# Output-weight sums in a hybrid attention layer: from accumulating DMAs to VectorE additions spread over three stages

## The chip, the cores and the metric

The kernel runs on one core of a Trainium2 chip. The metric is the device time of one execution in microseconds. The kernel before was timed in three runs; its time is their median. One further execution was profiled, and every row below is from that one.

## The reference

The reference is one layer of a streaming encoder: 16 learned meta tokens are put ahead of 512 positions of width 2048, and then

```python
u = rms_norm(h, pre_w)
proj = u @ w_in          # q, latent kv, gate, indexer for A; q, k, v, gate for B; two merge gates
# A: indexer scores, top-k keys per query, attention in the compressed space, 8 heads
# B: softmax(q1 k1 + bias) - lam * softmax(q2 k2 + bias) over a chunk mask, 8 heads, norm per head
y_a = (o_a * silu(z_a)) @ w_o_a
y_b = (o_b * silu(z_b)) @ w_o_b
mix = sigmoid(g_a) * y_a + sigmoid(g_b) * y_b
out = mix @ w_out
return h + rms_norm(out, post_w)
```

All in float32, 2048 columns in `mix` and `out`.

## The kernel before

The work goes in stages, one behind the other on TensorE: a first projection with the indexer, branch B (eight heads), branch A (eight heads), the gate stage, the merge, and the output product. float32 operands are split into a high and a low part, and a product is three matmuls.

**Fast products by seven.** The gate stage and the output product use the scheme that computes a 2x2 block product with seven block products in place of eight. The output product needs, of the weight `w_out` cut into blocks B11, B12, B21, B22, also four sums: T1 = B11 + B12, T3 = B12 + B22, T2 = T1 + B22 and T4 = T2 + B21 (the scheme's signs are taken up in other places). They depend on the weight alone. The kernel computes them on the chip, in 16 chunks of 128x512 elements (256 KB) for each sum, and stores them to the DRAM tensors `wout_t1` to `wout_t4` (line 80), from which the output stage loads them (lines 235 to 237) beside the plain blocks.

**How the sums are made before (lines 254 to 289).** `wt_chain` is a Python generator that handles one chunk. It loads two blocks into tiles of the pool `ogpool` through SyncE's DMA queue (line 265), has GpSimd's queue add other blocks of the weight onto them with accumulating DMAs (line 263, `accum_op=ALU.add`), and stores each sum as it stands through SyncE's queue (line 260). Load, add, store, add, store, add, store follow each other on the same tiles, so each waits for the one before to have landed. There are 16 chains with 2 loads, 4 accumulating DMAs and 4 stores each. Each DMA is pinned behind what was traced before it on its queue (`keep_in_program_order`); instructions that aren't pinned are ordered by a scheduler in the compiler, near the order in which they were traced. Two chains are alive at a time, and `wt_step` (line 284) moves both one step.

**Branch B (lines 889 to 907).** For each head there are three projections, for query, key and value, each in two halves. A projection's weights are a `Unit` (line 179): two raw loads of 512 KB through SyncE's queue (line 187), ScalarE's sum of squares of each (line 123), a reduction over partitions on GpSimd (line 128), a power-of-two scale from it on VectorE (lines 135 to 140), and the split into a high part on ScalarE and a low part on VectorE (lines 169 and 170). `advance` (line 205) brings one unit from one of these steps to the next at each half, so that one unit is split while the one before it is multiplied. Between the halves, pieces of the attention of the head before (`step`) and of branch A's top-k search on VectorE (`between`) are traced. One of the pieces transposes the probabilities on TensorE (line 683), which waits for VectorE's last combination of them (line 752).

**Gate stage (lines 1045 to 1081, run at line 1260).** 22 pairs of column blocks: two for what is left of branch A's gate, four for branch B's, sixteen for the merge gates; a pair is 7 products (`Pair.mm`, line 1006), a product is 24 matmuls (line 1019). A pair's raw loads go through SyncE's queue (line 1157), three of four into six shared slots; then squares, one reduction on GpSimd for a pair, a scale, VectorE's sums of blocks (line 1135) and the splits, three products ahead. `Run.run` traces, for each product n of 154: what is due (loads, bounds), the split for product n + 3, and, at each odd n, `wt_step`; then the product. ScalarE and VectorE take results out of PSUM (lines 1025 to 1039); branch outputs are loaded at lines 1103 and 1105 and gated ones stored at line 1118, on SyncE's queue as well.

**Merge (lines 1303 to 1326).** 16 steps, each with one product for A and one for B of 24 matmuls. For each product the weight is loaded three ahead (line 1236), reduced and split; the result is multiplied with its gate on VectorE (line 1320), and the two are added (line 1322). From step 8 on VectorE also forms sums of `mix` for the output product.

**Output product (lines 1421 to 1443).** Seven block products in the order 1, 2, 6, 7, 5, 3, 4; number 6 is the first that reads a stored sum.

Of the kernel before, what the change touches and what calls it, by code (L numbers as in the profile page):

```python
# [10 lines left out]
F32 = mybir.dt.float32  # L11
# [5 lines left out]
ALU = mybir.AluOpType  # L17
# [51 lines left out]
def layer_kernel(ctx, tc, xt_d, xn_d, cols_d, w0_d, wi_d, wkv_d, wo_d, wout_d, lam_d, post_d,  # L69
                 oh_d, rb_d, out_d):  # L70
    nc = tc.nc
# [3 lines left out]
    HB = [P, 512]  # L75
# [4 lines left out]
    tscr = [nc.dram_tensor(f"wout_t{i + 1}", [8, P, 1024], F32, kind="Internal").ap() for i in range(4)]  # L80
# [6 lines left out]
    opool = ctx.enter_context(tc.tile_pool(name="opool", bufs=1))  # L87
# [24 lines left out]
    def psum():  # L112
        return ps.tile([P, 512], F32, tag="a", name="acc")
# [91 lines left out]
    def advance(hf):  # L205

        q = units["now"]
        if hf == 0:
            units["use"] = q.pop(0)
            if q:  # L210
                q[0].scale()
        if q:
            q[0].split(hf)
        if len(q) > 1:
            q[1].bound(hf)
        if hf == 0 and units["todo"]:
            q.append(Unit(*units["todo"].pop(0)))
        return units["use"]
# [19 lines left out]
    state = {"raws": 0, "pos": 0, "ready": [], "stream": stream}  # L238
# [12 lines left out]
        assert key == (n, j, hf), (key, (n, j, hf))  # L251
        return hi, lo

    def wt_chain(k, n, tags):

        t = [state["ogpool"].tile(HB, F32, tag=tag, name="wt") for tag in tags]
        q = [[wout_d[ci, di, k, :, 512 * n:512 * n + 512] for di in range(2)] for ci in range(2)]

        def put(i, x):
            tc.keep_in_program_order(nc.sync.dma_start(tscr[i][k, :, 512 * n:512 * n + 512], x))  # L260

        def add(x, src):
            tc.keep_in_program_order(nc.gpsimd.dma_start(x, src, accum_op=ALU.add))  # L263
        for i in range(2):
            tc.keep_in_program_order(nc.sync.dma_start(t[i], q[0][i]))
        yield
        add(t[0], q[0][1])
        add(t[1], q[1][1])
        yield
        put(0, t[0])  # L270
        put(2, t[1])
        yield
        add(t[1], q[0][0])
        yield
        put(1, t[1])
        yield
        add(t[1], q[1][0])
        yield
        put(3, t[1])

    wt_todo = [(k, n) for k in range(8) for n in range(2)]
    wt_now = [None, None]

    def wt_step():
        for x in range(2):
            if wt_now[x] is None and wt_todo:
                wt_now[x] = wt_chain(*wt_todo.pop(0), [f"og{12 + 2 * x + y}" for y in range(2)])
            if wt_now[x] is not None and next(wt_now[x], "end") == "end":
                wt_now[x] = None

    def mm3(out, aH, aL, bH, bL, start, stop):
        nc.tensor.matmul(out, aH, bH, start=start, stop=False)  # L292
        nc.tensor.matmul(out, aH, bL, start=False, stop=False)  # L293
        nc.tensor.matmul(out, aL, bH, start=False, stop=stop)  # L294
# [11 lines left out]
    def proj_q(n, j):  # L306
        acc = psum()
        for hf in range(2):
            w = advance(hf)
            assert w.key == (n, j)  # L310
            for kk in range(8 * hf, 8 * hf + 8):
                mm3(acc, w.hi[:, kk], w.lo[:, kk], uH[kk][:, NM:T], uL[kk][:, NM:T],
                    kk == 0, kk == KT - 1)
            yield acc, w.un

    def proj_kv(n, j):
        acc = [psum(), psum()]
        for hf in range(2):
            w = advance(hf)
            assert w.key == (n, j)  # L320
            for t in range(2):
                s = slice(TH * t, TH * t + TH)
                for kk in range(8 * hf, 8 * hf + 8):
                    mm3(acc[t][:, :TH], w.hi[:, kk], w.lo[:, kk], uH[kk][:, s], uL[kk][:, s],
                        kk == 0, kk == KT - 1)
            yield acc, w.un
# [45 lines left out]
    def wide_f32(k, name):  # L372
        return upool.tile([P, T], F32, tag=f"u{k}", name=name)
# [9 lines left out]
    for kp in range(KT // 2):  # L383
# [19 lines left out]
        for k in (2 * kp, 2 * kp + 1):  # L403
            for j in range(3):
                for t in range(2):
                    s = slice(TH * t, TH * t + TH)
                    o = pc[j][:, t, :TH] if j < 2 else pik[t][:, :TH]
# [14 lines left out]
    for r in range(2):  # L422
        c = wide_f32(12 + r, "ckv")
# [120 lines left out]
    def stack64(psrc, scale, qpool, tag, bufs):  # L544
        q1 = qpool.tile([P, 512], F32R, tag=tag, name="q1", bufs=bufs)
        q2 = qpool.tile([P, 512], F32R, tag=tag, name="q2", bufs=bufs)
        a, b = (scale, scale) if isinstance(scale, float) else (scale[:64], scale[64:])
        nc.scalar.activation(q1[:64], psrc[:64], AF.Copy, scale=a)
        nc.scalar.activation(q2[64:], psrc[64:], AF.Copy, scale=b)
        nc.vector.scalar_tensor_tensor(q1[64:], psrc[:64], a, f32(q1[:64]),  # L550
                                       op0=ALU.mult, op1=ALU.subtract)
        nc.vector.scalar_tensor_tensor(q2[:64], psrc[64:], b, f32(q2[64:]),
                                       op0=ALU.mult, op1=ALU.subtract)
        return q1, q2
# [33 lines left out]
    for j in range(8):  # L588
        if j < 2:
            acc = piq[j]  # L590
# [50 lines left out]
    def run_topk(n):  # L641
        for _ in range(n):
            f = next(topk, None)
            if f is None:
                return
            f()
# [129 lines left out]
    def qstack(acc, un, h):  # L776

        q = stack64(acc, un, ap_, "q", 4)
        for m in range(2):
            hs = slice(64 * m, 64 * m + 64)  # L780
            nc.scalar.activation(QZ[h % 2][m][hs], acc[hs], AF.Copy, scale=un[hs])
        return list(q) + QZ[h % 2]
# [103 lines left out]
    def between():  # L886
        run_topk(TK.pop(0))

    for h in range(NH):
        for acc, un in proj_q("qb", h):  # L890
            step(2 if len(pending) == 7 else 1)
            between()
        q = qstack(acc, un, h)
        for acc, un in proj_kv("kb", h):
            step()
            between()
        kk = kstack(acc, un)
        if h == NH - 1:
            small_weights(0)
        for acc, un in proj_kv("vb", h):  # L900
            step()
            between()
        vt = ap_.tile([P, T], F32, tag="vt", name="vt", bufs=1)
        for t in range(2):
            nc.scalar.activation(vt[:, t * TH:(t + 1) * TH], acc[t][:, :TH], AF.Copy, scale=un)
        step(len(pending))
        pending = b_attend(h, q, kk, vt)
# [134 lines left out]
    QUADS = ("A11", "A21", "A12", "A22")  # L1042
    FIRST, ORDER = (1, 2, 5, 6, 3, 7), (1, 5, 0, 6, 2, 3, 7)

    class Run:


# [21 lines left out]
        def run(self, hooks=None):  # L1069
            for n in range(-2, 0):  # L1070
                for f in self.at.get(n, ()):
                    f()
            for n, (x, i) in enumerate(self.todo):
                for f in self.at.get(n, ()):
                    f()
                self.prep(n + self.ahead)
                for f in (hooks or {}).get(n - len(self.todo), ()):
                    f()
                if n % 2:
                    wt_step()  # L1080
                self.pairs[x].mm(i)

    ogpool = ctx.enter_context(tc.tile_pool(name="ogpool", bufs=1, reuse_waits="tile"))
# [89 lines left out]
    for i in list(range(NDIRECT, NH, 2)) + list(range(NH, 2 * NH, 2)):  # L1173
        def end(x, d, i=i):
            gate_o(i + x, d.o[x], d.r[x])
        n, c0 = ("za", i) if i < NH else ("zb", i - NH)
# [91 lines left out]
    yp = yg.enter_context(tc.tile_pool(name="yp", bufs=1, reuse_waits="tile"))  # L1268

    def load_sg(c):  # L1270
        t = []
        for ab in range(2):
            t.append(yp.tile(HB, F32, tag="sg", name="sg", bufs=6))
            nc.sync.dma_start(t[ab], sscr[ab][c])
        return t
# [28 lines left out]
    for c in range(KT):  # L1304
        sg = sgs.pop(0)
        if c + 2 < KT:
            sgs.append(load_sg(c + 2))
        for ab in range(2):
            key, _, _, (hi, lo, un) = wo_now.pop(0)
            assert key == (c, ab)  # L1310
            wo_load()
            wo_split(0)
            wo_bound(1)
            if not wo_now:
                state.update(pos=0, ready=[], stream=ystream)
                prefetch(1)
            acc = bank()
            for k in range(NH):
                mm3(acc, hi[:, k, :], lo[:, k, :], *OG[ab * NH + k], k == 0, k == NH - 1)
            nc.vector.scalar_tensor_tensor(sg[ab], acc, un, sg[ab], op0=ALU.mult, op1=ALU.mult)  # L1320
        mixf[c] = uk[c][0].tile([P, 512], F32, tag=uk[c][1], name="mix")
        nc.vector.tensor_add(mixf[c], sg[0], sg[1])
        if c >= 8:
            mix_sums(c - 8)
        if c >= 12:
            mix_prep(2)
# [94 lines left out]
    for x, i in enumerate(OUT_ORDER):  # L1421
        pool, tag = (ps, "a") if x % 2 else (ps2, "b")
# [89 lines left out]
```

## Time and profile before

| | |
|---|---|
| three runs | 1599.1, 1603.0, 1606.9 us; median 1603.0 |
| the profiled execution, its own time | 1607.0 us |
| its span, first to last instruction | 1605.2 us |
| mean granted TensorE clock | 0.964 |
| TensorE busy | 1442.2 us (90%) |
| VectorE busy | 1104.8 us (69%) |
| ScalarE busy | 978.7 us (61%) |
| GpSimd busy | 146.7 us (9%) |
| DMA | 257.3 MB, mean 160 GB/s |

PE is TensorE, DVE is VectorE, ACT is ScalarE, POOL is GpSimd, SP is SyncE; SPq and POOLq are the DMA queues that the last two issue. Matmuls overlap, so that TensorE's busy share says when it stood still and not how well it was used. The stages, by their first matmuls: branch B from about 130 us, branch A from about 515 us, the gate stage from 740 us, the merge from 1270 us, the output product from 1446 us.

### The profile page before, as it was taken

Reading aid. Unit: us, or ns where it says so; the run is one execution under the profiler, and the core shown is the slowest. Engines: PE = TensorE matmul, PEld = TensorE weight load, DVE = VectorE, ACT = ScalarE, POOL = GpSimd, SP = SyncE. Lnnn points to the kernel's source line nnn. Section 1 sums busy time; section 2 is a strip of 40 time slices with the busy share of each in tenths; the row PEclk is TensorE's granted clock in tenths of the full one; section 3 lists DMA queues with packets and bytes.
Section 4 is the critical chain, followed back from the end, with each engine's and each line's share of the span. In section 5 each row is a group of like instructions: output and inputs, shape, how many; then the busy total and the mean of one; then the engine's idle time right before and its main releaser. Section 6 shows DMA issues by size and latency. Waiting matters only on the chain. (4 is left out here: it accounts for less than half of the span.)

```text
span 1605.2 us, 25304 instructions
## 1 busy us (share of the span) xinstructions
PE 1442.2 (90%) x9475; PEld 1078.4 (67%) x9475; DVE 1104.8 (69%) x2091; ACT 978.7 (61%) x1735; POOL 146.7 (9%) x199
## 2 busy tenths in 40 slices
PE   7799998999999999999888677776999799999997
PEld 7678775677776666656777566665888544448885
DVE  7875767677775877857678455554778555656788
ACT  6364676676666877757667554644677644436555
POOL 3500100000000000001111111101000001100001
PEclk9899999999999999999999889888999999999999
DMA  6382332333322333237989967576544544447674
GB/s 209 119 296 86 119 100 86 100 99 100 98 85 83 112 106 107 93 122 223 257 243 276 256 173 205 167 208 182 158 132 145 189 153 157 149 126 262 226 250 153
DMA packets 104218, 257.27 MB, mean 160 GB/s; under 512 B 12072, under 2 KB 16392, under 8 KB 103968
## 3 DMA queue, kind: packets, MB, share of 16 engines
q1 hardware_dynamic: 86224, 223.86, 43.5%
q0 software_dynamic: 9216, 16.78, 6.1%
q10 hardware_dynamic: 8656, 15.02, 2.7%
q8 instruction: 74, 1.21, 0.3%
q14 instruction: 48, 0.39, 0.1%
HBM read 211.42 MB, written 47.41 MB: 161 GB/s over the span
## 5 line engine op out<-in xcount | busy, mean ns | idle before, releaser
L1019 PE MATMUL acc<-tu,wh 128*128 128x256 f16 x1408 | 254.5, 287 | 101.5 <-ACT q L1025 78.8
L1019 PEld LDWEIGHTS <-wh 128*128 128x128 f16 x2464 | 248.2, 101 | 142.2 <-issue 104.8
L123 ACT ACTIVATE junk<-raw 128x1024 bf16<-128x1024 f32 x192 | 202.2, 1053 | 187.5 <-DMA raw<-in_wi_dram 167.0
L292 PE MATMUL acc<-u,hi 128*128 128x264 f16 (+1 forms) x832 | 263.4, 317 | 0.7 <-DVE va L844 0.5
L294 PE MATMUL acc<-u,lo 128*128 128x264 f16 (+1 forms) x832 | 263.1, 316 | 0.0
L293 PE MATMUL acc<-u,hi 128*128 128x264 f16 (+1 forms) x832 | 263.1, 316 | 0.0
L170 DVE SCALAR_TENSOR_TENSOR wl<-S,scale,wh 128x1024 f16<-128x1024 f32 x88 | 112.8, 1283 | 140.3 <-ACT wh L169 140.3
L1019 PE MATMUL acc<-tu,wl 128*128 128x256 f16 x704 | 201.9, 287 | 0.0
L169 ACT ACTIVATE hi<-raw,scale 128x1024 f16<-128x1024 f32 x104 | 119.1, 1147 | 129.6 <-PE acc L293 128.4
L1019 PE MATMUL acc<-u,wh 128*128 128x256 f16 x1056 | 176.0, 273 | 0.0
L170 DVE SCALAR_TENSOR_TENSOR lo<-raw,scale,hi 128x1024 f16<-128x1024 f32 x104 | 132.8, 1280 | 51.3 <-ACT hi L169 51.0
L292 PEld LDWEIGHTS <-hi 128*128 128x128 f16 x1088 | 106.7, 98 | 78.8 <-issue 5.7
L294 PEld LDWEIGHTS <-lo 128*128 128x128 f16 x1088 | 106.7, 98 | 75.6 <-issue 0.8
L293 PEld LDWEIGHTS <-hi 128*128 128x128 f16 x1088 | 106.8, 98 | 71.9 <-issue 0.4
L1019 PE MATMUL acc<-u,wl 128*128 128x256 f16 x528 | 144.2, 273 | 1.5 <-DVE wl L170 1.5
L128 POOL PARTITION_ALL_REDUCE rows<-ssq x90 | 42.7, 474 | 1084.2 <-ACT junk L123 1052.9
L1019 PEld LDWEIGHTS <-wl 128*128 128x128 f16 x1232 | 124.3, 101 | 19.5 <-DVE wl L170 1.7
L169 ACT ACTIVATE wh<-S,scale 128x1024 f16<-128x1024 f32 x88 | 100.5, 1143 | 39.2 <-DVE S L1135 39.2
L292 PE MATMUL acc<-og,hi 128*128 128x512 f16 x256 | 97.3, 380 | 0.0
L293 PE MATMUL acc<-og,hi 128*128 128x512 f16 x256 | 97.1, 379 | 0.0
L294 PE MATMUL acc<-og,lo 128*128 128x512 f16 x256 | 97.0, 379 | 0.0
L170 DVE SCALAR_TENSOR_TENSOR wl<-raw,scale,wh 128x1024 f16<-128x1024 f32 x66 | 84.3, 1279 | 8.0 <-ACT wh L169 8.0
(313 smaller groups left out, 2898.4 us busy)
## 6 DMA issues: line engine op xcount, KB each, us to landing
raw<-in_wi_dram SPq DMA_DIRECT2D x172, 512.0 KB, 4.3
wt<-in_wout_dram POOLq DMA_DIRECT2D x64, 256.0 KB, 6.4
wout_t<-wt SPq DMA_DIRECT2D x64, 256.0 KB, 2.6
raw<-in_wo_dram SPq DMA_DIRECT2D x32, 512.0 KB, 6.3
raw<-wout_t SPq DMA_DIRECT2D x32, 512.0 KB, 3.6
raw<-in_wout_dram SPq DMA_DIRECT2D x24, 512.0 KB, 3.6
wt<-in_wout_dram SPq DMA_DIRECT2D x32, 256.0 KB, 5.9
sg<-r ACTq DMA_DIRECT2D x32, 256.0 KB, 2.0
```

The costliest lines, as they stand in the source:

```text
L123: nc.scalar.activation(j, src, AF.Square, accum_out=dst)
L128: nc.gpsimd.partition_all_reduce(r, ssq, P, bass_isa.ReduceOp.max)
L169: nc.scalar.activation(hi, src, AF.Copy, scale=s)
L170: nc.vector.scalar_tensor_tensor(lo, src, s, hi, op0=ALU.mult, op1=ALU.subtract)
L292: nc.tensor.matmul(out, aH, bH, start=start, stop=False)
L293: nc.tensor.matmul(out, aH, bL, start=False, stop=False)
L294: nc.tensor.matmul(out, aL, bH, start=False, stop=stop)
L1019: nc.tensor.matmul(acc, a[:, k, :], b, start=first and k == 0 and x == 0, stop=last and x == 2, skip_group_check=True)
```

## The change

The chains go. `wt_load` loads the four blocks of one chunk through SyncE's queue into four tiles, and `wt_sums` makes the four sums with VectorE additions in place, in an order in which each block is still whole when it is needed, and stores each through GpSimd's queue. A chunk is loaded and summed: in branch B once per head (loaded behind the query projection, summed behind the first half of the value projection, in tiles of `opool` that alternate between heads); in the gate stage four times (loaded at products 58, 76, 94 and 112, summed five products later, in the four `ogpool` tiles that the chains had); in the merge four times (loaded at steps 1, 4, 7 and 10, summed at the end of the following step, in four new tiles of the pool `yp`). The loads and stores are pinned; the additions are not. Nothing else changes.

```diff
-    def wt_chain(k, n, tags):
...
-    def wt_step():
...
+    wt = {"next": 0, "loaded": []}
+
+    def wt_load(pool, tags):
+        k, n = divmod(wt["next"], 2)
+        wt["next"] += 1
+        t = []
+        for tag, (ci, di) in zip(tags, ((0, 0), (0, 1), (1, 0), (1, 1))):
+            t.append(pool.tile(HB, F32, tag=tag, name="wt"))
+            d = nc.sync.dma_start(t[-1], wout_d[ci, di, k, :, 512 * n:512 * n + 512])
+            tc.keep_in_program_order(d)
+        wt["loaded"].append((k, n, t))
+
+    def wt_sums():
+
+        k, n, (b11, b12, b21, b22) = wt["loaded"].pop(0)
+        for i, (o, x) in ((0, (b11, b12)), (2, (b12, b22)), (1, (b22, b11)), (3, (b21, b22))):
+            nc.vector.tensor_add(o, o, x)
+            d = nc.gpsimd.dma_start(tscr[i][k, :, 512 * n:512 * n + 512], o)
+            tc.keep_in_program_order(d)
...
         q = qstack(acc, un, h)
+        wt_load(opool, [f"o{6 + 4 * (h % 2) + x}" for x in range(4)])
         for acc, un in proj_kv("kb", h):
...
-        for acc, un in proj_kv("vb", h):
+        for hf, (acc, un) in enumerate(proj_kv("vb", h)):
             step()
             between()
+            if hf == 0:
+                wt_sums()
...
+    WT_AT = (58, 76, 94, 112)
...
-                if n % 2:
-                    wt_step()
+                if n in WT_AT:
+                    wt_load(ogpool, [f"og{12 + y}" for y in range(4)])
+                if n - 5 in WT_AT:
+                    wt_sums()
                 self.pairs[x].mm(i)
...
+        if c in (1, 4, 7, 10):
+            wt_load(yp, [f"w{x}" for x in range(4)])
         for ab in range(2):
...
         nc.vector.tensor_add(mixf[c], sg[0], sg[1])
+        if c in (2, 5, 8, 11):
+            wt_sums()
```

## Rows read from the trace of the kernel before

**Rows 1.** Page part 2: the span in 40 equal slices, busy tenths.

```profile
PE   7799998999999999999888677776999799999997
...
PEclk9899999999999999999999889888999999999999
DMA  6382332333322333237989967576544544447674
```

**Rows 2.** Windows: us; PE, PEld, DVE, ACT, POOL busy (instructions); clock; DMA share; GB/s.

```profile
750.00:880.00 130.00, 112.50 (x989) 98.00 (x987) 96.55 (x118) 88.54 (x145) 24.21 (x30) 0.97 0.90 256
880.00:1133.00 253.00, 181.26 (x1494) 154.09 (x1493) 137.90 (x159) 131.12 (x197) 39.40 (x50) 0.86 0.73 198
1133.00:1235.00 102.00, 97.22 (x883) 86.10 (x881) 77.51 (x98) 72.59 (x108) 2.85 (x7) 1.00 0.42 139
310.00:510.00 200.00, 190.05 (x1382) 140.21 (x1381) 147.29 (x392) 131.93 (x256) 4.99 (x14) 1.00 0.31 94
1270.00:1445.00 175.00, 175.00 (x810) 82.32 (x809) 98.61 (x176) 70.35 (x98) 14.97 (x26) 0.98 0.47 148
```

**Rows 3.** GpSimd's timeline: start us, us, engine, line, operation, [idle before].

```profile
750.36 0.70 POOL L128 PARTITION_ALL_REDUCE rows<-ssq  x1 [19.14 <-ACT junk L123]
...
767.78 0.38 POOL L128 PARTITION_ALL_REDUCE rows<-ssq  x1 [0.71 <-ACT junk L123]
...
861.76 0.89 POOL L128 PARTITION_ALL_REDUCE rows<-ssq  x1
...
1125.59 0.37 POOL L128 PARTITION_ALL_REDUCE rows<-ssq  x1 [15.59 <-ACT junk L123]
...
1166.17 0.42 POOL L128 PARTITION_ALL_REDUCE rows<-ssq  x1 [19.95 <-ACT junk L123]
...
1224.15 0.42 POOL L128 PARTITION_ALL_REDUCE rows<-ssq  x1 [18.39 <-ACT junk L123]
```

**Rows 4.** Waits, 880 to 1133 us: us in total, times, longest us.

```profile
PE acc L1019 <- ACT q L1025: 64.8, 9, 11.9
...
ACT junk L123 <- DMA raw<-in_wi_dram: 93.3, 10, 14.6
...
SPq L260 <- DMA wt<-in_wout_dram: 117.8, 38, 6.8
SPq L1157 <- DVE r L1032: 91.1, 8, 14.2
```

**Rows 5.** Tile wt (ns min/median/max), and part 6 (us to landing last).

```profile
L263 POOL DMA_DIRECT2D wt<-in_wout_dram x64: 856/888/1940, 751.0 to 1126.6; - x64
L260 SPq DMA_DIRECT2D wout_t<-wt x64: 319/326/1542, 760.3 to 1132.7; - x64
...
wt<-in_wout_dram POOLq DMA_DIRECT2D x64, 256.0 KB, 6.4
...
wt<-in_wout_dram SPq DMA_DIRECT2D x32, 256.0 KB, 5.9
```

**Rows 6.** Waits, 1133 to 1235 us.

```profile
PE acc L1019 <- DVE r L1030: 3.0, 4, 1.3
...
SPq L1157 <- DVE r L1032: 45.7, 4, 12.0
```

**Rows 7.** Line 1322: ns min/median/max, first and last start us.

```profile
L1322 DVE TENSOR_TENSOR mix<-sg x16: 691/692/693, 1285.8 to 1441.2; 128x512 f32<-128x512 f32 x16
```

**Rows 8.** Timelines of TensorE and VectorE, a head of branch B.

```profile
340.22 1.07 PE L683 MATMUL acc<-ident,pr 128*128 128x128 f32 x8 [1.93 <-DVE pr L752]
...
382.76 1.07 PE L683 MATMUL acc<-ident,pr 128*128 128x128 f32 x8 [1.84 <-DVE pr L752]
...
416.92 0.16 DVE L135 TENSOR_REDUCE exp<-rows 128x1 f32<-128x2 f32 x1 [5.50 <-POOL rows L128]
```

**Rows 9.** Timelines of VectorE and TensorE, one step of the merge.

```profile
1307.11 1.28 DVE L170 SCALAR_TENSOR_TENSOR lo<-raw,scale,hi 128x1024 f16<-128x1024 f32 x1
...
1311.12 0.38 PE L294 MATMUL acc<-og,lo 128*128 128x512 f16 x1
```

More of the change, by code (lines that the diff above doesn't have):

```diff
@@ L252, in weights @@
         return hi, lo
-    def wt_chain(k, n, tags):
[L256 to L282, printed above, removed]
-    def wt_step():
[L285 to L289, printed above, removed]
+    wt = {"next": 0, "loaded": []}
[14 more added lines that the diff above has]
+            tc.keep_in_program_order(d)
     def mm3(out, aH, aL, bH, bL, start, stop):
```

## Prediction

> **What bounds the kernel now.** I read the page first: its slices show TensorE at 0.9 and more of nearly every slice, except for a trough from the 20th to the 28th slice (762 to 1123 us), where it falls to 0.6 to 0.8, the granted clock falls under full in most, and the DMA engines stand at 0.5 to 0.9 [rows 1]. That lies in the gate stage (lines 1045 to 1260), and it is just where the chunk chains of the old code run: their first GpSimd issue is at 751.0 us and their last store at 1132.7 us [rows 5].
>
> Next, windows over stages [rows 2]. From 880 to 1133 us TensorE is busy 181 of 253 us at a clock of 0.86; from 1133 to 1235 us, the same loop with the same pairs but no chain left, it is busy 97 of 102 us at 1.00. How long one pair takes is read from the one reduction that GpSimd makes for it [rows 3]: pairs 1 to 16 are 15 intervals from 750.36 to 1125.59 us, 375.2 us, 25.0 us each; the next five take 98.6 us, 19.7 each, and the last three of those 58.0 us, 19.33 each. A pair is 7 products of 24 matmuls; at full clock these are 97.22/883 = 0.110 us each [rows 2], so 168 of them are 18.5 us, the floor of a pair.
>
> Then, who waits [rows 4]. TensorE waits 64.8 us behind ScalarE's copy at line 1025, that is, on ScalarE being late; ScalarE waits 93.3 us for raw weights from DMA; and those loads stand in SyncE's in-order queue behind line 260, the chains' stores, which hold that queue for 117.8 us until an accumulating DMA has landed (6.4 us from issue [rows 5]). The trough is thus a queue: a store that waits for a slow transfer stands ahead of loads that could go. The other wait of that queue, 91.1 us of line 1157 for a free slot, is the loads running ahead; it also exists after 1133 us (45.7 us in 102 [rows 6]) where TensorE hardly waits, so it isn't the cause by itself.
>
> **What the change removes.** 16 chains, with 64 accumulating DMAs on GpSimd's queue, 64 stores on SyncE's and 32 loads there. In their place 16 chunks of 4 loads (64 on SyncE's queue), 4 VectorE additions and 4 stores (64 on GpSimd's queue). Transfers of 256 KB fall from 160 to 128, and only 4 chunks (32 transfers) are left in the gate stage. Nothing waits on SyncE's queue for a sum any more.
>
> Gate stage: 15 intervals at 25.0 us become 15 at the pace without chains. Bounds: 18.5 us (the floor, saves 375.2 - 277.5 = 97.7) and 19.71 us (all five, saves 79.5). I take 19.33, the last three, since the first two still work off what the chains left late: 375.2 - 290.0 = **85.2 us saved**. The first pairs of the stage also load branch outputs. With the chains they took (861.76 - 750.36)/5 = 22.3 us at a DMA share of 0.90 [rows 2, 3]; the first interval among them took 17.4 us, so they can hold this pace, and the chains' transfers go away.
>
> **What it adds.** One addition is 128x512 f32, as line 1322: 0.692 us [rows 7]. Four are 2.77 us of VectorE, 16 chunks 44.3 us. Bounds for each chunk: nothing, or 2.77 us in full. By stage:
>
> Branch B, eight heads, 22.1 us in all. VectorE is busy 147 of 200 us there [rows 2], so 11 us of a head's 42.5 us are idle. TensorE waits for it once a head, at the transposes of line 683, 1.84 us [rows 8]. The additions come right after those transposes, and before the next ones, 42.5 us later, VectorE sits idle 5.50 us for a GpSimd reduction which hangs on a raw load and not on VectorE [rows 8]. That wait is longer than 2.77 us: I take **0**. Without this cover it would be 22.1 us.
>
> Gate stage, four chunks, 11.1 us. VectorE is busy 77.5 of 102 us [rows 2], 4.6 us idle a pair, but for 3.0 us there TensorE waited for it [rows 6], so it has no full cover. Between 0 and 11.1 I take half, **5.5 us**.
>
> Merge, four chunks, 11.1 us. VectorE is busy 98.6 of 175 us [rows 2]. The additions come behind a mix addition of line 1322; the split behind that starts at 1307.11 and ends at 1308.39 us, and TensorE needs it at 1311.12 [rows 9], so 2.73 us are free against 2.77: I take **0**.
>
> The 64 stores: one GpSimd issue of this size took 0.888 us [rows 5], so four are 3.6 us of an engine that has little else to do, one behind each addition (0.692), and the reduction behind them comes some 1 to 2 us later than now. In branch B the split that hangs on it is made one unit ahead (42.5/3 = 14 us), so 0; bounds 0 and 16 x 3.6 = 57 us. The new wait is there: a store on GpSimd's queue waits for its addition, and that for the loads. The loads are traced a key projection, five products (13 us) or a merge step (10.4 us, 15 steps in 155.4 us [rows 7]) ahead of it, against 5.9 us to land [rows 5]. SyncE's queue gets 64 issues of 0.33 us instead of 96 of them: nothing. In branch B and merge the DMA share is 0.31 and 0.47 [rows 2]; 2 MB more a head or per three merge steps fits below the 0.90 seen. Output stage: its loads of the sums are as before, and the last store comes one merge step or more before the first such load: 0.
>
> **Sum.** -85.2 + 5.5 = -79.7 us on this execution's own 1607.0 us (span 1605.2 us and 1.8 around it): 1527.3. This execution stands 4.0 us above the median of 1603.0, so 1523.3 in terms of the median; I say 1524.
>
> A rule against part of the change: what the rows show is that SyncE's queue stood 117.8 us for chain stores [rows 4]. The Trainium skill's "DMA: Bandwidth & Descriptors", section "Issuing engines are not separate DMA queues", says that DMAs of all queues end on the same 16 engines, and that another issuing engine saves only the sequencer's issuing time. By that the stores' move alone would be worth 64 issues and the forecast would be rival 3's time.
>
> **Rivals.**
> 1. *The additions are on the path.* For: VectorE is 0.74 to 0.76 busy in branch B and gate stage. Against: the idle waits above. All 44.3 us instead of 5.5: 1562.
> 2. *The early pairs stay slow*, held by slots and by the branch outputs' loads, and only the pairs from 861.76 us on speed up. Then 5 x (22.3 - 19.33) = 15 us are not saved: 1538.
> 3. *The transfers, not the queue, set the pace.* 64 issues at 0.326 us [rows 5] are 21 us saved at most: 1582. For: DMA share 0.90 before 880 us. Against: 0.73 from 880 on, where the trough is deepest, and most bytes leave the stage.
> 4. *GpSimd's issue is starved by VectorE.* The issue has taken up to 1.940 us [rows 5]; if all do, four hold a reduction 7.8 us instead of 3.6, and 16 x 4.2 = 67 us fall on the path: 1590. Against: the median is 0.888 with VectorE busy over half of the time. The Trainium skill's "SBUF — State Buffer", section "SBUF: two separate sides", has this mechanism: some VectorE operations lock GpSimd out of a shared port, so that it cannot write descriptors.
> 5. *Slower: the loads come late.* SyncE's queue is in order, so chunk loads may stand behind a raw load which waits for a slot, up to 12.0 us in the stretch without chains [rows 6]; then VectorE stands at the additions, with every split behind them, and TensorE behind the splits. 16 x 12.0 = 192 us more: 1715. It decides from 79.7/16 = 5.0 us a chunk. Against: the loads are issued behind a fetch whose slots come free about two products later, some ten products before the additions.
>
> **How the numbers follow.** Forecast 0.82; rivals 1 and 2 0.05 each; 3 0.03; 4 0.02; 5 0.03. The range reaches down to the floor pace with free additions (-97.7: 1505) less 3 us, most of the 3.9 by which the fastest run shown lies under the median, and up to near rival 1: 1502 to 1558. Left out are rivals 3 to 5 and part of 1. 0.5% (8 us) is about what a measurement of this kernel can tell from no change. Faster by more: forecast, rivals 1 to 3, 0.95; within: rival 4, whose time is 5 us from that bound, 0.02; slower: rival 5, 0.03.
>
> **What would show it.** Right: reductions of the gate stage about 19.3 us apart from the start, granted clock 1.00 there, no line 260 wait, ScalarE's 93.3 us for raw weights down to a small part; a head of branch B still 42.5 us; merge at 10.4 us a step. Wrong: pairs of 25 us (the queue was not the cause), a longer head (additions or reductions late), VectorE waits for the chunk's loads (rival 5), or GpSimd issues near 2 us (rival 4).

## The result, and the profile after

The changed kernel took 1532.7 us (median of 4 runs, 1528.9 to 1539.4), the kernel before beside it on the same chip 1605.0 us (4 runs): a ratio of 0.9555, 95% interval 0.9501 to 0.9608. The prediction of 1524 us (0.951 of its 1603) lies inside that interval and the result inside its range. The profiled execution took 1536.0 us, its span 1534.2.

The page of the changed kernel, parts 2, 3 and 6, against [rows 1, 5]:

```profile
PE   7799997989999999999999989999998899999996
...
PEclk9899999999999999999999999999999999999998
DMA  6383374434545333332656554545446566556773
...
q0 software_dynamic: 5120, 16.78, 3.0%
...
wt<-in_wout_dram SPq DMA_DIRECT2D x64, 256.0 KB, 5.1
wout_t<-wt POOLq DMA_DIRECT2D x64, 256.0 KB, 3.1
```

The trough of the gate stage is gone from all three rows: TensorE and its clock stand at 9 in nearly every slice there, the DMA engines at 4 to 6 where they stood at 5 to 9. Windows of the changed kernel, against [rows 2] (same columns; the gate stage in two parts, branch B, the merge):

```profile
763.00:894.00 131.00, 124.42 (x1123) 109.86 (x1121) 112.16 (x135) 105.48 (x171) 3.35 (x8) 1.00 0.52 165
894.00:1050.00 156.00, 146.25 (x1315) 128.96 (x1314) 123.33 (x145) 110.27 (x165) 9.44 (x20) 0.99 0.51 167
...
310.00:510.00 200.00, 187.74 (x1317) 135.16 (x1318) 154.07 (x396) 127.45 (x248) 14.38 (x30) 0.98 0.45 140
1205.00:1373.00 168.00, 166.22 (x765) 76.32 (x763) 105.76 (x192) 68.43 (x97) 22.25 (x42) 1.00 0.58 194
```

In the gate stage TensorE is 94 to 95% busy at a clock of 0.99 to 1.00, where the deepest part of the trough had 181 of 253 us at 0.86 [rows 2]. GpSimd's reductions for pairs 1, 16 and 21 in the changed kernel, against [rows 3]:

```profile
763.57 0.70 POOL L128 PARTITION_ALL_REDUCE rows<-ssq  x1 [19.15 <-ACT junk L123]
...
1049.57 0.37 POOL L128 PARTITION_ALL_REDUCE rows<-ssq  x1 [17.20 <-ACT junk L123]
...
1148.60 0.42 POOL L128 PARTITION_ALL_REDUCE rows<-ssq  x1 [18.40 <-ACT junk L123]
```

With them, and the output product's first matmul on a `wt` tile (1446.1 us before, 1373.4 after; its very first matmuls start 6.1 and 6.0 us earlier, so the 1446 us in the list of stages is this one too), the span falls into five stretches:

| stretch | before | after | difference |
|---|---|---|---|
| start to pair 1 (first projection, both branches) | 750.4 | 763.6 | +13.2 |
| pair 1 to pair 16, 15 intervals | 375.2 | 286.0 | -89.2 |
| pair 16 to pair 21 | 98.6 | 99.0 | +0.5 |
| pair 21 to that matmul (merge) | 221.9 | 224.8 | +2.9 |
| that matmul to the end | 159.1 | 160.8 | +1.7 |
| span | 1605.2 | 1534.2 | -71.0 |

The waits of the changed kernel from 763 to 1050 us, against [rows 4]:

```profile
ACT junk L123 <- DMA raw<-in_wi_dram: 15.4, 9, 3.0
PE acc L1005 <- DVE r L1016: 9.4, 11, 2.2
PE acc L1005 <- ACT q L1011: 6.9, 10, 1.9
...
DVE wt L270 <- DMA wt<-in_wout_dram: 3.3, 3, 1.4
```

and of SyncE's queue in the same stretch:

```profile
SPq L1147 <- DVE r L1018: 97.7, 10, 12.1
```

ScalarE's 93.3 us of waiting for raw weights are 15.4, TensorE's 64.8 us behind ScalarE's copy are 6.9. No chunk load or store has a row among the waits of SyncE's queue. The queue's wait for a free slot, 91.1 us before [rows 4], is still there with 97.7 us, while ScalarE hardly waits for raw loads. The raw loads (line 1157, now 1147) land in a median of 4.0 us, at most 5.1 (before 5.2, at most 9.9; both from 755 to 1130 us).

What was gained there was partly lost in the branches. Six heads of branch B, from the transposes at 253.09 us to those at 510.24, took 257.2 us; now, from 254.60 to 520.92, they take 266.3, 9.2 more.

### The profile page after: what moved, and what is told of

It reads as the page before. It is cut to its first block, busy times and chain, and to the rows that moved or that the text cites. A ratio compares the mean times of both kernels' runs of the same rounds, so it can differ in the third digit from the quotient of the medians.

```text
span 1534.2 us, 25341 instructions
## 1 busy us (share of the span) xinstructions
PE 1431.7 (93%) x9475; PEld 1070.6 (70%) x9475; DVE 1141.9 (74%) x2155; ACT 980.7 (64%) x1735; POOL 123.6 (8%) x199
## 3 DMA queue, kind: packets, MB, share of 16 engines
q0 software_dynamic: 5120, 16.78, 3.0%
## 4 chain that ended last, share of the span: by engine, by line
issue 31%; PE 26%; DVE 16%; DMA 14%; ACT 9%; POOL 2%; SPq 1%; ACTq 0%; POOLq 0%; DVEq 0%
DMA raw<-in_wi_dram 8%; PE acc L275 5%; PE acc L277 4%; PE acc L276 4%; DVE lo L170 4%; ACT junk L123 3%; PE acc L1411 3%; PE acc L1413 3%; PE acc L1412 3%; DMA wt<-in_wout_dram 2%; DVE wl L170 2%; POOL rows L128 2%; DMA raw<-in_wo_dram 2%; ACT wh L169 1%; ACT hi L169 1%
## 5 line engine op out<-in xcount | busy, mean ns | idle before, releaser
L1005 PEld LDWEIGHTS <-wh 128*128 128x128 f16 x2464 | 242.2, 98 | 68.0 <-issue 38.6
L1005 PE MATMUL acc<-tu,wh 128*128 128x256 f16 x1408 | 237.8, 275 | 32.4 <-DVE r L1016 22.1
L1005 PE MATMUL acc<-tu,wl 128*128 128x256 f16 x704 | 193.9, 275 | 0.0
L1005 PEld LDWEIGHTS <-wl 128*128 128x128 f16 x1232 | 121.1, 98 | 14.6
```

Of the source, the lines that this page charges most:

```text
L1005: nc.tensor.matmul(acc, a[:, k, :], b, start=first and k == 0 and x == 0, stop=last and x == 2, skip_group_check=True)
```

## The experiments

The theory was that a store which waits for a slow accumulating transfer holds up SyncE's queue. The first question was what share of the gate stage's 88.8 us (pairs 1 to 21: 473.8 us before, 385.0 after) that is, against the slow transfers themselves and their number; the second, where branch B's 9 us come from. "Pairs 1 to 21" below is read from GpSimd's reductions as above, one execution each.

### A later store

Edit of the kernel before: one more step between each of three adds and its store, and more steps to make up for it.

```diff
         add(t[1], q[1][1])
         yield
+        yield
         put(0, t[0])
...
-                if n % 2:
+                if n % 2 or n % 20 == 0:
```

> The kernel before, its chains as they are, with one more step between each accumulating DMA and the store of its sum, so that a store comes up on SyncE's queue when its sum has landed; the chains then take most of the gate stage. Same transfers, same queues. If the queue held by waiting stores is what makes the trough, pairs take 19 to 21 us, the 20 intervals from pair 1 to 21 fall from 473.8 us to 390 to 415 us, the line of the stores waits under 20 us, and the time is 1530 to 1555 us. If the transfers themselves set the pace, they are only spread out: the 20 intervals stay at 450 us or more and the time is 1580 us or more.

Measured: 1614.4 us (1612.3 to 1616.9), a ratio of 1.0063 [1.0046, 1.0079]; pairs 1 to 21 took 453.8 us. SyncE's queue from 752 to 1205 us:

```profile
SPq L260 <- DMA wt<-in_wout_dram: 146.0, 47, 7.8
```

The edit missed its aim. The store still waits 146 us in all: SyncE runs ahead of the compute, so it comes to the store early wherever the store is traced. The trough is spread out, not gone. Both numbers lie in the expectation's second range, but the wait that the edit was to remove is still there, so nothing follows about the cause.

### Stores that wait for nothing

Edit of the kernel before: the 64 stores write a constant tile; number, size and place of all transfers stay.

```diff
-        put(0, t[0])
-        put(2, t[1])
+        put(0, state["cst"])
+        put(2, state["cst"])
...
-        put(1, t[1])
+        put(1, state["cst"])
...
-        put(3, t[1])
+        put(3, state["cst"])
```

(Beside this, the chains take turns on two sets of tiles, so that a chain's first loads wait for no older add. And GpSimd's adds no longer wait until a store has read their tile, 116.3 us in all from 755 to 1130 us before; that held up no reduction to speak of, as VectorE waited 3.5 us for reductions in that stretch.)

> The kernel before with its 160 transfers, but the 64 stores write a constant tile, so that they need not wait for an accumulating DMA (the sums are thus not stored), and the chains' tiles alternate, so that loads wait less too. If SyncE's queue, held by the waiting stores (117.8 us between 880 and 1133 us before), makes the trough, the line of the stores waits for nothing, pairs take 19 to 21 us and the 20 intervals from pair 1 to 21 fall from 473.8 us to 395 to 420 us, the time to 1530 to 1560 us. If the transfers set the pace, whichever queue they wait in, the intervals stay above 450 us and the time above 1580 us. The run before this one showed why a later store is no test: SyncE comes to it early anyway, and waited 159 us.

Measured: 1572.7 us (1568.3 to 1573.7), a ratio of 0.9796 [0.9773, 0.9818]. Its reductions for pairs 1 and 21:

```profile
755.92 0.70 POOL L128 PARTITION_ALL_REDUCE rows<-ssq  x1 [19.12 <-ACT junk L123]
...
1191.73 0.42 POOL L128 PARTITION_ALL_REDUCE rows<-ssq  x1 [18.51 <-ACT junk L123]
```

and its waits from 755 to 1130 us:

```profile
ACT junk L123 <- DMA raw<-in_wi_dram: 59.8, 12, 8.7
...
PE acc L1019 <- ACT q L1025: 36.4, 13, 6.2
```

Line 260 has no wait left in SyncE's queue, and pairs 1 to 21 take 435.8 us: 38.0 of the 88.8 us. ScalarE still waits 59.8 us for raw weights (93.3 in the same stretch before), which land in a median of 5.4 us, at most 11.0, and TensorE 36.4 us on ScalarE (76.8 before). Pairs and time both lie between the expectation's two ranges. So the held queue is a cause, and not the only one.

### Plain copies instead of accumulating ones

Edit of the kernel before, the queue's hold left as it is:

```diff
-            tc.keep_in_program_order(nc.gpsimd.dma_start(x, src, accum_op=ALU.add))
+            tc.keep_in_program_order(nc.gpsimd.dma_start(x, src))
```

> The kernel before with the 64 accumulating DMAs of GpSimd's queue made plain copies (the sums are thus not made); chains, waits, stores and queues as before. If what hurt is that accumulating transfers are slow (6.4 us to land, 6.1% of the DMA engines' time for 16.8 MB), the 20 intervals fall from 473.8 us to 420 us or less and the time to 1560 us or less. If it is the waiting in SyncE's queue whatever the transfer, the wait shrinks only with the landing, from 6.4 to some 4 us, and the intervals stay at 430 to 460 us, the time at 1565 to 1590 us.

Measured: 1577.6 us (1577.4 to 1579.5), a ratio of 0.9834 [0.9814, 0.9854]. Reductions for pairs 1 and 21:

```profile
751.57 0.70 POOL L128 PARTITION_ALL_REDUCE rows<-ssq  x1 [19.13 <-ACT junk L123]
...
1196.55 0.42 POOL L128 PARTITION_ALL_REDUCE rows<-ssq  x1 [18.53 <-ACT junk L123]
```

Part 3 of its page, and SyncE's queue from 755 to 1130 us:

```profile
q0 software_dynamic: 5120, 16.78, 3.0%
```

```profile
SPq L260 <- DMA wt<-in_wout_dram: 98.4, 41, 6.5
```

Pairs 1 to 21 take 445.0 us, 28.8 less than before, though the stores still hold the queue for 98.4 us (128.2 us in the same stretch before). The same 16.78 MB cost GpSimd's queue 3.0% of the DMA engines' time instead of 6.1%, and land in 5.2 us instead of 6.5 (medians of that stretch). Both numbers lie in the expectation's second range, in which the hold only gets shorter; whether the slow transfer costs something beside it is the next run's question.

### Both at once

Edit: the last two together.

> The kernel before with the edits of the two runs before it together: the 64 stores write a constant tile, so that nothing on SyncE's queue waits for a transfer, and the 64 accumulating DMAs are plain copies (the sums are left out). The number, size and place of all 160 transfers stay. From pair 1 to pair 21 the kernel before took 473.8 us, the changed one 385.0; the constant stores alone gave 435.8 (38 us less), the plain copies alone 445.0 (29 us less). Theory: the held queue and the accumulating transfers are two costs of their own, and the sum of both is saved: 473.8 - 38 - 29 = 407 us from pair 1 to 21, a time of 1606 - 33 - 28 = 1545 us, a ratio of 0.962; what is left up to the changed kernel's 385 (22 us) is the number of transfers in the stage. Rival 1, one cost seen twice (the queue is held because the accumulating transfer is slow): no better than the better of the two, 436 us and 1573 us, 0.98; then the 128 transfers that leave the stage have the remaining 50 us. Rival 2, the transfers' number costs nothing once queue and accumulation are out: 385 us, 1524 us, 0.95.

Measured: 1551.5 us (1548.6 to 1553.1), a ratio of 0.9657 [0.9632, 0.9682]. Reductions for pairs 1 and 21, then the wait for raw weights from 755 to 1130 us:

```profile
757.69 0.70 POOL L128 PARTITION_ALL_REDUCE rows<-ssq  x1 [19.12 <-DMA wt<-in_wout_dram]
...
1169.27 0.42 POOL L128 PARTITION_ALL_REDUCE rows<-ssq  x1 [18.59 <-ACT junk L123]
```

```profile
ACT junk L123 <- DMA raw<-in_wi_dram: 45.7, 15, 6.5
```

ScalarE's wait for raw weights shrinks again (59.8 and 71.1 us in the two before), and it is 411.6 us from pair 1 to 21: 62.2 us less than before, where the two alone gave 38.0 and 28.8, 66.8 together. They are two costs of their own; rival 1 of the expectation (one cost seen twice, 436 us) is out, and rival 2 (385 us) too. What is left to the changed kernel, 26.6 us, is left with all 160 transfers of 256 KB in the stage instead of 32, and raw loads still land later here (median 4.6 us, at most 8.8, against 4.0 and 5.1). That fits the number of transfers, but no run changed the number alone. The time is 6.5 us over the 1545 expected; pair 1 comes 7.3 us later than before, in branches that the edit does not touch. That also shows in the run with constant stores alone (5.6 us), and why was not tried. So a later pair 1 alone doesn't show a cost in branch B.

### Branch B's eight chunks in the gate stage

Edit of the changed kernel: no chunk in branch B, twelve in the gate stage.

```diff
-        wt_load(opool, [f"o{6 + 4 * (h % 2) + x}" for x in range(4)])
...
-            if hf == 0:
-                wt_sums()
...
-    WT_AT = (58, 76, 94, 112)
+    WT_AT = tuple(range(8, 140, 11))
```

> The changed kernel with the eight chunks of branch B moved into the gate stage, twelve there, every eleven products. If the gate stage gained by getting rid of the held queue and not by losing transfers, its 20 intervals stay near the 385.0 us of the changed kernel, plus at most 2.77 us for each of eight chunks: 385 to 407 us; if it gained because twelve of sixteen chunks left it, they go back above 420 us. Branch B gets back to the six head periods of before, 257 us against 266, and the first pair's reduction to about 753 us against 763.6. Time by the first 1525 to 1545 us, by the second 1550 us or more.

Measured: 1551.4 us (1549.1 to 1553.9), a ratio of 0.967 [0.9652, 0.9687]. Pair 1 comes at 752.70 us (763.57 with the chunks in branch B), and the six heads take 256.7 us, as before the change. Pairs 1 to 21 take 411.0 us, 26.0 more, between the two ranges expected: 3.2 us for each of the eight chunks more, against 10.9 us (1.4 each) for all eight in branch B. The medians are 18.7 us apart, and the two intervals don't meet, so this placement is slower. That need not be the stage's doing alone. Waits of SyncE's queue and of VectorE from 753 to 1164 us:

```profile
SPq L262 <- DMA wout_t<-wt: 31.9, 15, 4.8
```

```profile
DVE wt L270 <- DMA wt<-in_wout_dram: 30.2, 16, 5.3
```

Twelve chunks in a row share four tiles. A chunk's loads wait until the chunk before has been stored, 31.9 us in all, and hold SyncE's queue meanwhile; in the changed kernel they have no row among that queue's waits from 755 to 1130 us. VectorE then stands 30.2 us for loads that come late (4.3 us in the changed kernel's pairs 1 to 21), the prediction's rival 5 in small. How much of the 26.0 us is that, and how much the additions (2.77 us a chunk) or the transfers, was not separated.

### Branch B's additions left out

Edit of the changed kernel: branch B's loads and stores stay, its 32 additions go.

```diff
-    def wt_sums():
+    def wt_sums(add=True):
...
-            nc.vector.tensor_add(o, o, x)
+            if add:
+                nc.vector.tensor_add(o, o, x)
...
-                wt_sums()
+                wt_sums(add=False)
```

> The changed kernel without the additions of branch B's eight chunks (blocks are loaded and stored unsummed, so half of the sums are left out). If VectorE's additions cost branch B its 9 us, the six head periods fall to 257 to 260 us; if it is the chunk's transfers that delay the raw loads, they stay at 263 us or more. Time 1522 to 1528 us by the first, 1529 us or more by the second.

Measured: 1530.3 us (1526.4 to 1534.5), a ratio of 0.9542 [0.9522, 0.9563]. The six heads take 260.6 us (254.23 to 514.85), between the two ranges expected, and pair 1 comes at 756.71. TensorE's waits over the six heads in the kernel before, in the changed one and in this one:

```profile
PE acc L683 <- DVE pr L752: 17.0, 7, 6.2
```

```profile
PE acc L666 <- DVE pr L735: 17.1, 7, 6.3
PE s L729 <- DVE mx L656: 5.9, 5, 2.4
```

```profile
PE acc L667 <- DVE pr L736: 17.1, 7, 6.3
...
PE s L730 <- DVE mx L657: 0.4, 1, 0.4
```

The wait at the transposes is the same in all three. New in the changed kernel is a wait at the logits (line 729) for PSUM that VectorE's softmax has yet to read, 5.9 us; without the additions it is 0.4. By the traces, then, the additions cost some 6 us in the six heads (266.3 against 260.6) and 7 up to pair 1.

The 3.4 us that are left over the 257.2 before look like the transfers' cost, but they are not shown to be. The six heads in the kernel before, in the changed one, in this one, and in the run "Both at once", which has no chunk in branch B (columns as in [rows 2], the clock a mean over the stretch):

```profile
253.09:510.24 257.15, 244.89 (x1765) 181.73 (x1765) 187.02 (x506) 170.23 (x330) 6.42 (x18) 0.99 0.31 94
```

```profile
254.60:520.92 266.32, 248.47 (x1764) 182.30 (x1765) 204.24 (x532) 171.58 (x330) 19.97 (x42) 0.98 0.45 140
```

```profile
254.23:514.85 260.62, 248.00 (x1765) 183.86 (x1765) 187.58 (x508) 169.79 (x330) 19.32 (x42) 0.98 0.45 144
```

```profile
253.68:513.64 259.96, 248.02 (x1764) 184.00 (x1765) 187.23 (x506) 170.09 (x330) 6.38 (x18) 0.98 0.31 94
```

Without the additions TensorE stands still as little as before (12.6 us against 12.3), and the 3.4 us are its own busy time, 248.0 us instead of 244.9, at a granted clock of 0.98 instead of 0.99. "Both at once" shows the same 248.0 without any chunk there. Of the changed kernel's 9.2 us, 3.6 are busy time of this kind and 5.6 standing still. In the medians the additions are worth only 2.4 us, and the two intervals overlap: these are single executions, 3.3 us over the median (changed) and 1.0 under it (this one).

VectorE's timeline of the changed kernel in one such place:

```profile
305.80 0.16 DVE L135 TENSOR_REDUCE exp<-rows 128x1 f32<-128x2 f32 x1 [1.89 <-POOL rows L128]
...
306.39 0.69 DVE L270 TENSOR_TENSOR wt<-wt 128x512 f32<-128x512 f32 x1
307.66 1.42 DVE L270 TENSOR_TENSOR wt<-wt 128x512 f32<-128x512 f32 x2 [0.58 <-DMA wt<-in_wout_dram]
...
310.19 0.68 DVE L270 TENSOR_TENSOR wt<-wt 128x512 f32<-128x512 f32 x1
310.80 0.30 DVE L656 CUSTOM_DVE_ANT_0 pr<-s,G 128x144 f32<-128x144 f32 x1
```

The additions stand not in the idle time ahead of the reduction's result but behind it, right before the softmax that TensorE waits for (2.38 us, until 311.16). They aren't pinned, so the scheduler placed them.

### The additions one key projection later, then pinned into the idle time

Two edits of the changed kernel. In the first the additions are traced in the next head's key projection:

```diff
+        for hf, (acc, un) in enumerate(proj_kv("kb", h)):
+            if hf == 1 and h > 0:
+                wt_sums()
...
-            if hf == 0:
+            if hf == 0 and h == NH - 1:
```

> The changed kernel with branch B's sums traced a head later and before the last softmax block, where VectorE waits for a reduction, in place of behind the transposes. If the loss in branch B is that the additions lie where VectorE is just about to read the next head's first logits, and that the loads land late, the six head periods fall from 266.3 to 257 to 260 us and the time to 1522 to 1529 us. If the additions or the transfers cost the same wherever they lie, the heads stay at 264 to 268 us and the time within 4 us of 1533.

Measured: 1535.0 us (1530.9 to 1538.7), 0.9566 [0.9546, 0.9587], six heads 266.6 us. Another miss: the scheduler put them behind the scale again (308.81 us). So the second edit pins them besides:

```diff
-            nc.vector.tensor_add(o, o, x)
+            a = nc.vector.tensor_add(o, o, x)
+            if pin:
+                tc.keep_in_program_order(a)
```

> As the run with branch B's sums traced a head later, but the additions are pinned behind what is traced before them on VectorE; in the run without the pin the scheduler had put them back behind the scale, ahead of the next softmax. If their place is what cost, TensorE's waits for the logits' banks (5.9 us over six heads in the changed kernel) go, the six head periods fall from 266.3 to 257 to 261 us and the time to 1523 to 1530 us. If additions cost the same anywhere, the heads stay above 264 us and the time within 4 us of 1533.

Measured: 1532.1 us (1528.6 to 1533.6), 0.9545 [0.9523, 0.9567]. VectorE in one head, and TensorE's waits over the six:

```profile
326.91 2.87 DVE L270 TENSOR_TENSOR wt<-wt 128x512 f32<-128x512 f32 x4
333.16 0.15 DVE L135 TENSOR_REDUCE exp<-rows 128x1 f32<-128x2 f32 x1 [3.39 <-POOL rows L128]
```

```profile
PE acc L668 <- DVE pr L737: 22.5, 7, 6.4
```

Now the four additions do stand in the idle time, with 3.39 us of it to spare, and the wait at the logits is gone. But the wait at the transposes grew from 17.1 to 22.5 us, and the six heads take 266.4 us (253.33 to 519.68), as before the edit. The wait moved and nothing was gained. The last of the seven transposes, on TensorE, and what VectorE did just before:

```profile
519.68 1.94 PE L668 MATMUL acc<-ident,pr 128*128 128x128 f32 x8 [4.70 <-DVE pr L737]
```

```profile
518.80 0.11 DVE L650 MEMSET G<- 64x64 f32 x1 [2.93 <-DMA G<-bias_rows]
```

Of the 5.5 us more than in the kernel before (17.0), 3.1 lie in this one place (1.64 us there), where VectorE stood 2.93 us for a bias load; whether the chunks delayed that load was not tried. The other six waits are 0.2 to 0.6 us longer than before each, and why is open. TensorE's busy time in the six heads was 249.0 us, at a clock of 0.97.

### The stores on SyncE's queue

Edit of the changed kernel:

```diff
-            d = nc.gpsimd.dma_start(tscr[i][k, :, 512 * n:512 * n + 512], o)
+            d = nc.sync.dma_start(tscr[i][k, :, 512 * n:512 * n + 512], o)
```

> The changed kernel with the 64 stores on SyncE's queue in place of GpSimd's. If a store that waits in SyncE's queue delays the raw loads behind it, the gate stage's 20 intervals grow from 385.0 us by 5 to 20 us, branch B's heads by some us, and the time is 1540 to 1560 us. If additions are soon enough done that the queue hardly waits, the time stays within 4 us of 1533 and the queue that stores go through was not a part of the gain.

Measured: 1528.8 us (1527.8 to 1530.5), 0.9526 [0.9507, 0.9546]; pairs 1 to 21 took 385.8 us (762.12 to 1147.93). The queue that the stores go through is no part of the gain once VectorE makes the sums: the stores held SyncE's queue for 10.5 us over the whole run, and none waits for an accumulating transfer. "DMA: Bandwidth & Descriptors" of the Trainium skill, section "Issuing engines are not separate DMA queues", says that moving DMAs to another issuing engine saves only the sequencer's time to start them; this run agrees, with 1528.8 us against 1532.7 and intervals that overlap.

### Seven chunks in the merge

Edit of the last one, to beat both: three of the gate stage's four chunks go to the merge.

```diff
-    WT_AT = (58, 76, 94, 112)
+    WT_AT = (58,)
...
-        if c in (1, 4, 7, 10):
+        if c in (0, 2, 4, 6, 8, 10, 12):
...
-        if c in (2, 5, 8, 11):
+        if c in (1, 3, 5, 7, 9, 11, 13):
```

> The changed kernel with the 64 stores on SyncE's queue, and three of the gate stage's four chunks moved into the merge, which then has seven (loads at steps 0, 2, 4 to 12, additions one step later); branch B keeps its eight. Theory: a chunk costs what the stages showed, 3.2 us in the gate stage (8 more chunks there were 26 us) and 0.7 us in the merge (4 chunks, 2.9 us): 3 x 3.2 = 9.6 us saved and 2.2 us lost, 1529 - 7 = 1521 to 1522 us, and 375 us from pair 1 to pair 21. Rival 1, the gate stage with four chunks is at its own pace already and the cost grows only beyond them: 385 us from pair 1 to 21, 1529 to 1531 us. Rival 2, the sums of the last steps come too late for the output stage's loads, and TensorE waits at its start: 1535 us and more, with a TensorE wait of over 5 us at the stage's start that the changed kernel doesn't have.

Measured: 1531.1 us (1528.3 to 1534.3), 0.9536 [0.9513, 0.9559]. Reductions for pairs 1 and 21, then TensorE's waits from 1130 us on:

```profile
766.41 0.70 POOL L128 PARTITION_ALL_REDUCE rows<-ssq  x1 [19.12 <-ACT junk L123]
...
1145.66 0.42 POOL L128 PARTITION_ALL_REDUCE rows<-ssq  x1 [18.46 <-ACT junk L123]
```

```profile
PE acc L277 <- DVE lo L170: 5.0, 7, 1.3
```

The gate stage gained 6.6 us (379.3 from 385.8), 2.2 a chunk, where 9.6 were expected; and pair 21 to the output product's first matmul on a `wt` tile took 227.5 us instead of 221.6 (1369.57 less 1147.93 in the run before), 5.9 us more where 2.2 were expected. The wait for a late split, 5.0 us, had no row in the run before. What is gained in one stage is lost in the other; no version measured is faster than the changed kernel by more than the intervals allow.

## Why the prediction was right, and where it was off

- **Gate stage: right in kind and size.** Forecast for pairs 1 to 16 was 290.0 us plus 5.5 for additions, measured 286.0: 9.5 us better. (The additions of the fourth chunk start at 1055.61 us, behind pair 16; over pairs 1 to 21, where all four lie, it is 9.1.) The pace is 19.07 us a pair, between the floor of 18.5 and the 19.33 taken. Two sizes offset each other here: by the run with seven chunks in the merge a chunk costs the stage 2.2 us, so four are 8.8 instead of 5.5, and the pace without chunks is then about 18.8 us, (385.0 - 8.8)/20, an estimate. The early pairs speeded up with the rest (rival 2 is out: pairs 1 to 6, 763.57 to 858.10 at 18.9 us each).
- **"The trough is thus a queue": only a part.** The forecast named one cause. The experiments show two, the held queue with 38 us and the accumulating transfers' own cost with 29 (together 62 of the 89), and leave 27 that fit the number of transfers, which was not tested alone. The saving came out right because it was taken from the pace of pairs without any chain, which lacks all of them. Rival 3 put the queue at 21 us by its 64 issues; the run with constant stores keeps all of these issues and saves 38 us in the stage.
- **Branch B at 0: the step that failed.** The cover was real (5.50 us of idle VectorE [rows 8]), but the unpinned additions were put elsewhere, and pinning them into it gained nothing. The prediction looked for the cost at the transposes; it came up at the logits, 5.9 us. The six heads lengthened by 9.2 us, against 16.6 if all of their additions had been on the path (six of eight heads of rival 1's 22.1). Without the additions they took 260.6 us; the 3.4 us left are TensorE at a lower clock, which a kernel without chunks there shows as well, so that the transfers cost anything in branch B is not shown. Over the whole time up to pair 1 the term is +13.2 by these profiles, 10.9 of it branch B's chunks by the run without them; but kernels without chunks there reach pair 1 between 750.4 and 757.7 us, so single microseconds of this mean little.
- **Merge at 0: near.** +2.9 us in the profile, with waits for the split of 1.7 us in all (four times, at most 0.8); with the stores on SyncE's queue it was 221.6 us, as before. The cover of 2.73 us against 2.77 held about as well as its narrowness said.
- **GpSimd's issues (rival 4): out.** A store's issue took 0.542 us in the median and at most 0.866, less than the 0.888 of the accumulating ones.
- **Late chunk loads (rival 5): out for this kernel.** VectorE waited 3.3 us for them in the gate stage up to 1050 us. With twelve chunks there it was 30.2 us.
- The sum was -79.7 and the span gave -71.0: 9.5 us better up to pair 16, 18.2 worse elsewhere. That the forecast lies so near the result is in part these errors offsetting each other.

## What to carry to other kernels

Where a stage is starved, take its pace from a stretch of the same loop without the suspected work: that gave the right saving even though the cause had more than one part. An idle stretch of an engine isn't yet a cover: the scheduler must put the work there, and with short slack all around, a wait that is taken from one place comes up at another. A store that needs a transfer's result, put ahead of loads in an in-order queue, costs more than its issue time: here 38 us of a stage on top of 21 us of issues.

## What was not expected of the hardware

A short wait of TensorE costs more than itself. Windows around its 2.38 us wait at the logits, changed kernel:

```profile
308.00:310.00 2.00, 0.77 (x7) 0.55 (x5) 1.97 (x3) 1.23 (x3) 1.08 (x2) 1.00 0.49 182
310.00:312.00 2.00, 0.84 (x3) 0.38 (x4) 2.00 (x7) 0.86 (x4) 0.54 (x1) 1.00 0.85 250
312.00:314.00 2.00, 2.00 (x6) 0.51 (x5) 2.00 (x9) 1.14 (x4) 0.00 (x0) 0.66 0.76 249
314.00:316.00 2.00, 2.00 (x6) 0.68 (x5) 1.29 (x5) 1.04 (x2) 0.00 (x0) 0.50 1.04 415
```

After two windows with TensorE 0.77 and 0.84 of 2.00 us busy, the granted clock is 0.66 and then 0.50, that is 1.2 instead of 2.4 GHz; from 316 us on it is back at 0.99. The two windows lose (0.34 + 0.50) x 2.00 = 1.7 us of full-clock time on top of the wait.

How soon a store of 256 KB landed did not go by its queue (medians of 64): from SyncE's 2.6 us in the kernel before, 5.1 and 3.4 in the last two runs, from GpSimd's 3.1 in the changed kernel and 4.8 with twelve chunks in the gate stage. And the same bytes took twice the share of the DMA engines (6.1% against 3.0%) when they were added to their destination.
